# A two-layer decoder trunk on one core: transfers taken off ScalarE's queue, a fixed order for the sums of activations, and one product's loop order

## The chip, the cores and the metric

The kernel runs on one core of one Trainium2 chip. The metric is the device time of one execution in microseconds (us); of each kernel several executions are timed and the median is given. Beside these, one execution is recorded by the profiler; its span and trace are what is read below.

## The reference, cut to what matters

Two decoder layers are applied to a prompt of 1024 tokens and to 8 samples of 4 new tokens, together 1056 columns, with a model width of 1024.

- Layer 0 mixes tokens by attention in three dilated windows per head (12 pairs of head and window), whose outputs are combined by softmax denominators. Layer 1 mixes by a state space: the projected input u goes through 32 groups of 64 complex states and out again as y, then through a GELU and a gated product ("GLU").
- In both layers four heads of cross-attention read 256 memory tokens, and one output projection merges mixer and cross-attention into the residual x.
- Each layer ends in a gated FFN of width 2816, with a causal convolution of width 3 between up-projection and activation: `(silu(a) * b) @ w_down`.
- Everything is float32. Each dense product is made of three passes on TensorE, each operand split into a high part (a cast to fp32r) and a low part (the rest).

Outputs are the two activations, the new key and value windows, the new states and the convolution's last rows.

## The kernel before

**Engines and queues.** TensorE (PE) does all products and transposes. ScalarE (ACT) makes the high parts, exponentials and most copies out of PSUM; VectorE (DVE) the low parts, reductions and residual sums; GpSimd (POOL) some low parts and elementwise products. Each engine runs its instructions in the order in which the program lists them. Transfers are issued from three queues: SyncE (SP) issues weights and most reloads; POOL issues cache reads and window outputs; ACT issues what it has just written: attention outputs (`og`, `xm`, `xo`), the state space's output (`d_y`), states and convolution rows, 155 transfers in all. A transfer's issue stands in the engine's list like any instruction: what comes behind it waits until it is issued.

**Planner.** `Meter` (L112 to L198) keeps an estimated clock per engine while the program is written; `pump` (L329) moves pieces of side work, kept in 14 lanes, between the matmuls of the dense products when their inputs are estimated to be ready. So the order of each engine's list follows from estimated costs; a transfer on POOL is put at 1.0 us, on SP or ACT at 0.05 us.

**Attention (layer 0).** `scores` (L1138) works on two blocks at a time: scores on PE, maximum on DVE, exponential on ACT, transposes on PE, copies on ACT, product on PE, copy on ACT, then the write to `og`. `combine_head` reads `og` back, combines, and writes `xm`. `cross_p` and `cross_s` do cross-attention and write `xo`. Tiles S (14 buffers) hold the scores' data until the write has landed.

**State space (layer 1).** For each quarter m of the 32 groups, `s5_u_evac` (L1753) writes u to memory (`d_u`) and reads it back transposed into `s5u` in 8 transfers, both on SP. `s5_states` makes the states on PE, ACT copies them out of PSUM, DVE rotates and scans them; `s5_out` (L1821) makes y on PE, applies GELU on ACT and writes `d_y` in 8 transfers on ACT's queue. Between these, PE works on the cross-attention's projections. Four PSUM buffers (`pm`) serve the side work.

**FFN.** The first 3 of 22 tiles of the up-projection are made plainly, the others by a Strassen-like scheme with 7 products (`up_tiles`, L2160) that needs sums of quarters of the normalized activations: `t1`, `t2` (split into high and low), `t3`, `t4`. `up_moving` (L2065) makes the sums on DVE as side work of a lane, a step wherever the planner finds DVE free, in the stretch of the plain tiles. Product 0 uses unsummed activations, product 1 uses `t2` and product 2 adds to product 0's PSUM buffers, after ACT has copied product 0 out.

**Output projection.** `out_half` (L1918) makes 8 tiles of 128 rows; `dense` (L422) goes over three chunks of 352 columns with the k-blocks inside, or, with `along`, over the k-blocks with the chunks inside.

Of the kernel before, what the change touches and what calls it, by code (L numbers as in the profile page):

```python
# [10 lines left out]
F32 = mybir.dt.float32  # L11
# [3 lines left out]
ALU = mybir.AluOpType  # L15
AX = mybir.AxisListType

P = 128
# [93 lines left out]
class Meter:  # L112
# [51 lines left out]
    def note(self, eng, op, args, kw):  # L164
        outs = [kw[k] for k in ("out", "accum_out") if kw.get(k) is not None] or [args[0]]
        ins = list(args["out" not in kw:]) + [v for k, v in kw.items() if k not in ("out", "accum_out")]
        ins = [a for a in ins if hasattr(a, "tensor")]
        out = outs[0]
        n = out.free_size()
        src = next((a for a in ins if a.free_size() >= n), out)  # L170
        start = max(self.t[eng], self.ready(ins, eng), *(self.used.get(o.tensor.name, 0.0) if o.space == bass.MemoryType.PSUM else 0.0 for o in outs))
        if op == "dma_start":
            if out.space != bass.MemoryType.DRAM:
                start = max(start, self.t["tensor"] - 4.0)
            self.t[eng] = start + (1.0 if eng == "gpsimd" else 0.05)
            self.dma[eng] = max(self.dma.get(eng, 0.0), self.t[eng] + 1.6) + n * out.ap[0][1] * 4 / 350e3
            end = self.dma[eng] + 0.2
        else:
            if eng == "tensor":
                wide = ins[0].dtype == F32  # L180
                turn = op == "transpose"
                cost = 0.107 if turn else max(n * 4 / 2400 + 0.008, 0.107) + 0.03 if wide else max(n / 2400, 0.025) + 0.0025
            elif eng == "scalar":
                vecs = sum(hasattr(kw.get(x), "tensor") for x in ("scale", "bias", "accum_out"))
                cost = (0.051 if src.space == bass.MemoryType.PSUM else 0.094) + n * 0.833e-3 + 0.0935 * vecs
            elif eng == "gpsimd":
                cost = 0.147 + n * 2.105e-3
# [61 lines left out]
class Kernel:  # L249
# [661 lines left out]
    def cross_p(self, h, b0, q, a, done, kmt, kv, dst):  # L911
# [5 lines left out]
        for st in range(b0, b0 + 5):  # L917
# [18 lines left out]
            if st < b0 + 4:  # L936
# [9 lines left out]
                nc.scalar.copy(out=t, in_=p2[:, 0, :])  # L946
                self.m.let_go(p2)
                yield t
        nc.scalar.dma_start(out=dst[:, b0 * P:(b0 + 4) * P], in_=q[:, b0 * P:(b0 + 4) * P])
        self.crossed += 1  # L950

    def cross_s(self, l, qs, sqs, dst, ring_of, lane=None):
# [83 lines left out]
        o2 = self.M()  # L1036
        nc.scalar.copy(out=o2, in_=po[:, 0, :])
        for h in range(4):
            nc.scalar.dma_start(out=dst[h][:, NPR:], in_=o2[:, h * 32:(h + 1) * 32])
        self.crossed += 1  # L1040

    def cross_heads(self, lanes, heads, cq, kmt, kv, xo):
# [95 lines left out]
    def scores(self, g, h, part, qT, kT, vt):  # L1138
# [8 lines left out]
        for j in (part, part + 2):  # L1147
# [31 lines left out]
            nc.scalar.copy(out=o[:, :, 0:P], in_=po[:, 0:2, :])  # L1179
            self.m.let_go(po)  # L1180
            if g == 0:
                nc.scalar.dma_start(out=og.rearrange("(b p) x -> p b x", p=P)[:, 2 * j:2 * j + 2, :], in_=o)
            elif g == 1:
                nc.scalar.dma_start(out=og.rearrange("(e p r) x -> r p e x", p=P, r=4)[j], in_=o)
            else:
                v = og.rearrange("(l j e r) x -> r j l e x", j=4, e=2, r=2)
                for r in range(2):
                    nc.scalar.dma_start(out=v[r, j], in_=o[r * 64:(r + 1) * 64])
            del t, o
        self.scored[h] += 1  # L1190

# [6 lines left out]
    def combine_head(self, h, halves=(0, 1)):  # L1198
        while self.scored[h] < 6:
            yield WAIT  # L1200
        for i in halves:
            x01, x2 = self.combine_load(h, i)
            row = self.B((P, 512))
            yield DVE, x01, x2
            yield from self.combine(row, x01, x2)
            self.nc.scalar.dma_start(out=self.xm[h][:, i * 512:(i + 1) * 512], in_=row)
            del x01, x2, row
            self.scored[h] += 1

# [543 lines left out]
    def s5_u_evac(self, m, i, ps):  # L1753
# [23 lines left out]
        nc.sync.dma_start(out=win, in_=self.d_win[:, m * 4:m * 4 + 4])  # L1777
        nc.sync.dma_start(out=rot, in_=self.d_rot[:, m * 4:m * 4 + 4])
        for tau in range(8):
            nc.sync.dma_start(out=self.s5u[tau * 16:(tau + 1) * 16, m * 8:m * 8 + 8], in_=uv[tau][:, m * 8:m * 8 + 8])  # L1780
        self.lanes[0].append(self.s5_states(m, win, rot))

    def s5_states(self, m, win, rot):
# [37 lines left out]
    def s5_out(self, m, tl, cl):  # L1821
# [17 lines left out]
        nc.scalar.activation(out=y, in_=y, func=AF.Gelu_apprx_tanh)  # L1839
        yv = self.d_y.rearrange("(g c) t x -> t c g x", c=16)  # L1840
        for tau in range(8):
            nc.scalar.dma_start(out=yv[tau][:, m * 8:m * 8 + 8, :], in_=y[tau * 16:(tau + 1) * 16])
        self.s5_done += 1

    def s5_final(self):
# [20 lines left out]
        self.nc.tensor.transpose(ps[:32, 0, :], fin, self.ident)  # L1866
        po = self.M((32, P))
        nc.scalar.copy(out=po, in_=ps[:32, 0, :])
        nc.scalar.dma_start(out=self.O["p_s5"][0, 0].rearrange("r (i e) p -> (r i) (e p)", e=2), in_=po)
        for hf in range(2):  # L1870
            so = self.B((16, 8, P))
            for q in range(2):
                yield sf
                ps = self.pm((P, 4, P))
                for w in range(4):
                    self.nc.tensor.transpose(ps[:16, w, :], sf[:, hf * 8 + q * 4 + w].rearrange("p b r -> p (b r)"), self.ident)
                nc.scalar.copy(out=so[:, q * 4:q * 4 + 4, :], in_=ps[:16])
            nc.scalar.dma_start(out=self.O["s_s5"][0].rearrange("b r g p -> (b r) (g p)")[:, hf * D:(hf + 1) * D], in_=so.rearrange("p a b -> p (a b)"))

    def y_load(self, m):  # L1880
        y = self.B()
# [36 lines left out]
    def out_half(self, kt, aat, ahead=3, deep=1):  # L1918
        for m in range(8):
            self.wdeep = deep if m > 5 else 1  # L1920
            for j in range(m, min(m + ahead, 8)):
                self.reload_x(j)
            ps = self.dense_w(kt, aat)
            self.residual(m, ps)

    def cross_gather(self, xo, l):
# [85 lines left out]
    def conv_store(self, l):  # L2012
        nc = self.nc
        so = self.O["s_conv"][l].rearrange("b j c -> (b j) c")
        for q, last in ((0, 7), (3, 9), (1, 15), (4, 17), (2, 21), (5, 21)):
# [10 lines left out]
                nc.scalar.copy(out=r[:, hf * 4:hf * 4 + 4, :], in_=ps[:18])  # L2026
                self.m.let_go(ps)
            rv = r.rearrange("p a b -> p (a b)")
            nc.scalar.dma_start(out=so[:, q * D:q * D + n * P], in_=rv[0:16, :n * P])
            nc.scalar.dma_start(out=self.O["p_conv"][l, 0, :, q * D:q * D + n * P], in_=rv[16:18, :n * P])  # L2030
        self.cst = None

    def conv_sb(self, ct, u, out):
# [31 lines left out]
    def up_moving(self):  # L2065

        nc, y = self.nc, self.x
        tt = nc.vector.tensor_tensor
        L, R = slice(0, HT2), slice(HT2, NT)
        t1, t2 = self.mv = [self.L((P, 2, 4, HT2), F32R) for _ in range(2)]  # L2070
        for k in range(4):
            u, v = y[k], y[k + 4]
            yield DVE, u
            tt(out=u[:, L], in0=u[:, R], in1=u[:, L], op=ALU.subtract)
            nc.scalar.copy(out=t1[:, 0, k, :], in_=u[:, L])
            yield DVE
            tt(out=u[:, R], in0=v[:, R], in1=u[:, R], op=ALU.subtract)
            yield DVE
            tt(out=v[:, R], in0=v[:, R], in1=u[:, L], op=ALU.subtract)
            nc.scalar.copy(out=t2[:, 0, k, :], in_=v[:, R])  # L2080
            yield DVE
            tt(out=t1[:, 1, k, :], in0=u[:, L], in1=t1[:, 0, k, :].bitcast(F32), op=ALU.subtract)
            yield DVE
            tt(out=v[:, L], in0=v[:, L], in1=v[:, R], op=ALU.subtract)
            yield DVE
            tt(out=t2[:, 1, k, :], in0=v[:, R], in1=t2[:, 0, k, :].bitcast(F32), op=ALU.subtract)
        self.moving = True

    def up_raw(self, l, ht, s):
        if ht < NHT:  # L2090
# [69 lines left out]
    def up_tiles(self, l, weights):  # L2160
# [15 lines left out]

        def split_t3():
            for k in range(4):
                self.split_to(y[k][:, R], h0[:, k, R], l0[:, k, R])
                yield  # L2180

        def split_t4():
# [101 lines left out]
    def ffn(self, l, *side):  # L2284
        nc = self.nc
        first = [None] * 2
        self.hd, self.hid, self.uraw, self.uops, self.moving = {}, {}, {}, deque(), False
        self.wend = self.wi + 2 * PLAIN

        def evac(s, i, ps):  # L2290
# [7 lines left out]
                pass  # L2298

        h = self.norm_dense(FCG, evac)  # L2300
        self.lanes[1].append(self.up_moving())
        last(0, first)
        del first
        weights = self.up_weights(l)
# [1 line left out]
        for ht, s in ((ht, s) for ht in range(1, PLAIN) for s in range(2)):  # L2306
# [8 lines left out]
            for i in range(3):  # L2315
                ps = self.dense(8, lambda k: (hi[:, k, :], lo[:, k, :]), h, FCG[i:i + 1])[0]
                self.pump()
                if todo:
                    self.conv(*todo.pop())
                    if len(ab) == 3:  # L2320
                        last(ht - 1, (ab.pop(0), ab.pop(0)))
# [3 lines left out]
        del ab, ps, hi, lo  # L2325
        self.up_raw(l, PLAIN + 1, 1)
        h = None
        self.until(lambda: self.moving)
        late = self.up_tiles(l, weights)
        self.nh = None  # L2330
        for g in range(5):
# [287 lines left out]
```

## Time and profile before

| | |
|---|---|
| timed runs | 2921.52, 2922.92, 2925.99 us; median 2922.92 us |
| profiled execution | 2920.49 us, of which span 2918.7 us |
| mean granted TensorE clock | 0.971 of full speed |
| busy, share of the span | PE 94%, PEld 90%, DVE 70%, ACT 42%, POOL 13% |
| transfers | 431.56 MB, mean 148 GB/s |

The share of busy time tells which engine sets the time on average; what a change of one stage is worth is read from the waits in that stage. Times in the rows are in us from the span's start, unless they are marked ns. Nearly every instruction has line L216, since a helper issues it; groups are told apart by the tiles that they write and read (B<-pd is a tile B written from a PSUM tile pd).

### The profile page before, as it was taken

How to read it: one execution, taken by the hardware profiler on the slowest of the kernel's cores; microseconds unless marked ns; L12 is line 12 of the kernel's file. 1: busy time of each engine (PE TensorE's matmuls, PEld its weight loads, DVE VectorE, ACT ScalarE, POOL GpSimd, SP SyncE). 2: the span in 40 equal slices, each digit the busy share in tenths (PEclk: the TensorE clock that was granted, in tenths of full speed). 3: DMA queues.
4: the chain of work that ended last, by engine and by line, in shares of the span. 5: the costliest groups of instructions: out<-in, count | busy, mean ns of one | idle time of the engine just before them, and what ended most of it. 6: DMA issues, size and time to landing. Idle time of an engine off the chain costs nothing.

```text
span 2918.7 us, 50794 instructions
## 1 busy us (share of the span) xinstructions
PE 2734.6 (94%) x18896; PEld 2620.0 (90%) x18896; DVE 2055.1 (70%) x5933; ACT 1220.0 (42%) x3045; POOL 388.2 (13%) x571
## 2 busy tenths in 40 slices
PE   7999989999889999999999899888999999999999
PEld 5999878898878999999999888677999999999998
DVE  7466876887786787878769776545478787876444
ACT  5555555455441544444431124246244444443211
POOL 2100121112012400000102456000140000000000
PEclk8999999999989999999999999999999999999999
DMA  7234756757473423433564335853443233346421
GB/s 248 84 94 132 213 166 206 203 169 208 147 218 122 157 88 117 124 117 124 171 223 139 137 104 164 239 135 117 150 147 124 95 124 117 124 132 230 157 81 67
DMA packets 377348, 431.56 MB, mean 148 GB/s; under 512 B 31191, under 2 KB 331253, under 8 KB 375677
## 3 DMA queue, kind: packets, MB, share of 16 engines
q1 hardware_dynamic: 333212, 362.13, 39.0%
q0 software_dynamic: 20816, 50.04, 5.7%
q10 hardware_dynamic: 23072, 16.14, 2.0%
q8 instruction: 149, 2.44, 0.3%
q14 instruction: 99, 0.80, 0.1%
HBM read 345.10 MB, written 172.37 MB: 177 GB/s over the span
## 4 chain that ended last, share of the span: by engine, by line
PE 30%; DVE 22%; ACT 8%; issue 3%; DMA 2%; POOL 0%; ACTq 0%; SPq 0%; POOLq 0%; DVEq 0%
PE pd L216 26%; DVE B L216 18%; ACT B L216 5%; PE pm L216 4%; DVE S L216 3%; ACT S L216 1%; ACT L L216 1%; DVE A L216 0%; DMA B<-in_w_down 0%; DVE T L216 0%; DMA d_cl<-S 0%; DVE L L216 0%; ACT T L216 0%; ACT A L216 0%; DMA d_u<-M 0%
## 5 line engine op out<-in xcount | busy, mean ns | idle before, releaser
L216 PE MATMUL pd<-A,B 128*128 128x352 f32 (+2 forms) x10992 | 1791.2, 317 | 46.5 <-DVE B L216 31.0
L216 PEld LDWEIGHTS pd<-A,B 128*128 128x128 f32 x10992 | 1648.4, 191 | 74.9 <-issue 38.1
L216 DVE TENSOR_TENSOR B<-B,B 128x512 fp32r<-128x512 f32 (+7 forms) x612 | 514.5, 849 | 222.3 <-ACT B L216 212.2
L216 ACT CAST B<-B 128x512 fp32r<-128x512 f32 (+4 forms) x430 | 313.8, 751 | 671.7 <-DVE B L216 349.2
L216 PE MATMUL pd<-L,B 128*128 128x264 f32 (+1 forms) x2976 | 448.5, 303 | 14.1 <-DVE L L216 9.2
L216 PEld LDWEIGHTS pd<-L,B 128*128 128x128 f32 x2976 | 416.8, 190 | 18.1 <-DVE L L216 9.8
L216 DVE TENSOR_TENSOR B<-pd,B 128x352 f32<-128x352 f32 x408 | 203.0, 520 | 205.5 <-PE pd L216 198.2
L216 ACT COPY B<-pm 128x512 f32<-128x512 f32 (+5 forms) x261 | 129.7, 507 | 206.1 <-PE pm L216 203.0
L216 PE MATMUL pd<-B,B 128*128 128x264 f32 (+2 forms) x1308 | 205.5, 307 | 6.8 <-DVE B L216 6.8
L216 DVE SCALAR_TENSOR_TENSOR B<-B,S,B 128x1023 f32<-128x1023 f32 (+1 forms) x152 | 194.3, 1278 | 0.0
L216 PEld LDWEIGHTS pd<-B,B 128*128 128x128 f32 x1308 | 182.7, 191 | 11.1 <-ACT L L216 6.7
L216 PE MATMUL pm<-const,B 128*128 128x128 f32 (+6 forms) x1119 | 163.2, 276 | 26.7 <-DMA B<-in_g_mix 7.3
L216 PEld LDWEIGHTS pm<-const,B 128*128 128x128 f32 (+4 forms) x1119 | 132.4, 149 | 46.3 <-issue 17.3
L216 ACT COPY S<-pm 128x256 f32<-128x256 f32 (+5 forms) x278 | 89.1, 349 | 164.9 <-PE pm L216 154.5
L216 ACT COPY B<-pd 128x352 f32<-128x352 f32 (+4 forms) x211 | 104.2, 542 | 102.3 <-PE pd L216 95.2
L216 ACT CAST A<-B 128x352 fp32r<-128x352 f32 (+3 forms) x148 | 97.7, 669 | 114.0 <-DVE B L216 48.1
L216 ACT ACTIVATE B<-B 128x352 f32<-128x352 f32 (+3 forms) x127 | 94.3, 750 | 62.3 <-DVE B L216 58.5
L216 PE MATMUL pm<-const,S 128*128 128x128 f32 (+3 forms) x464 | 80.7, 283 | 33.6 <-ACT S L216 22.7
L216 DVE SCALAR_TENSOR_TENSOR L<-L,T,L 128x128 f32<-128x128 f32 x404 | 108.3, 346 | 4.0 <-DMA L<-in_cache_win_kv 3.9
L216 DVE CUSTOM_DVE_ANT_0 M<-L,L 128x128 f32<-128x128 f32 x384 | 94.6, 306 | 16.9 <-ACT M L216 6.1
L216 PEld LDWEIGHTS pm<-const,S 128*128 128x128 f32 (+2 forms) x464 | 58.3, 155 | 48.7 <-ACT S L216 30.2
L216 ACT ACTIVATE B<-B,S 128x1056 f32<-128x1056 f32 x76 | 96.7, 1273 | 2.4 <-DVE B L216 2.4
(217 smaller groups left out, 2503.1 us busy)
## 6 DMA issues: line engine op xcount, KB each, us to landing
B<-in_w_up SPq DMA_DIRECT2D x88, 512.0 KB
hd<-B SPq DMA_DIRECT2D x44, 528.0 KB
B<-hd SPq DMA_DIRECT2D x44, 528.0 KB
B<-in_w_down SPq DMA_DIRECT2D x44, 512.0 KB
B<-in_w_in_a SPq DMA_DIRECT2D x40, 512.0 KB
B<-xsp SPq DMA_DIRECT2D x32, 528.0 KB
L<-in_cache_win_kv SPq DMA_DIRECT2D x16, 1024.0 KB
L<-in_cache_win_kv SPq DMA_DIRECT2D x64, 256.0 KB
```

The costliest lines, as they stand in the source:

```text
L216: return f(*args, **kw)
```

## The change

Three things are changed, beside one cost of the planner (0.6 instead of 1.0 us for a transfer on POOL).

1. All 155 transfers of ACT's queue are issued by POOL. The reads of u into `s5u` (32) go from SP to POOL.
2. `up_moving` is no lane any more. It is stepped by the loop over the plain tiles, once after each of 12 dense products (the first step only takes the buffers, 8 steps work). `t3` is now formed from `t2`, and `t3` and `t4` are made on POOL (8 subtractions of 528 columns per layer). DVE keeps 16 of its 24; ACT's 8 copies stay.
3. The first tile of each `out_half` runs with `along`.

```diff
-            self.t[eng] = start + (1.0 if eng == "gpsimd" else 0.05)
+            self.t[eng] = start + (0.6 if eng == "gpsimd" else 0.05)
...
     # cross_p, cross_s, scores, combine_head, s5_out, s5_final, conv_store
-        nc.scalar.dma_start(out=dst[:, b0 * P:(b0 + 4) * P], in_=q[:, b0 * P:(b0 + 4) * P])
+        nc.gpsimd.dma_start(out=dst[:, b0 * P:(b0 + 4) * P], in_=q[:, b0 * P:(b0 + 4) * P])
...
     # s5_u_evac
         for tau in range(8):
-            nc.sync.dma_start(out=self.s5u[tau * 16:(tau + 1) * 16, m * 8:m * 8 + 8], in_=uv[tau][:, m * 8:m * 8 + 8])
+            nc.gpsimd.dma_start(out=self.s5u[tau * 16:(tau + 1) * 16, m * 8:m * 8 + 8], in_=uv[tau][:, m * 8:m * 8 + 8])
...
     # s5_out
         for tau in range(8):
-            nc.scalar.dma_start(out=yv[tau][:, m * 8:m * 8 + 8, :], in_=y[tau * 16:(tau + 1) * 16])
+            nc.gpsimd.dma_start(out=yv[tau][:, m * 8:m * 8 + 8, :], in_=y[tau * 16:(tau + 1) * 16])
...
     # out_half
-            ps = self.dense_w(kt, aat)
+            ps = self.dense_w(kt, aat, along=m == 0)
...
     # up_moving, inner part
+        yield
+        for step in ("a0", "a1 p0", "a2 p1", "a3 p2", "b0 p3", "b1", "b2", "b3"):
+            for w in step.split():
+                k = int(w[1])
+                u, v = y[k], y[k + 4]
+                if w[0] == "a":
+                    tt(out=u[:, R], in0=u[:, R], in1=u[:, L], op=ALU.subtract)
+                    tt(out=v[:, R], in0=v[:, R], in1=u[:, R], op=ALU.subtract)
+                    nc.scalar.copy(out=t1[:, 0, k, :], in_=u[:, R])
+                    nc.scalar.copy(out=t2[:, 0, k, :], in_=v[:, R])
+                elif w[0] == "p":
+                    nc.gpsimd.tensor_tensor(out=u[:, L], in0=v[:, R], in1=u[:, L], op=ALU.subtract)
+                    nc.gpsimd.tensor_tensor(out=v[:, L], in0=v[:, L], in1=v[:, R], op=ALU.subtract)
+                else:
+                    tt(out=t1[:, 1, k, :], in0=u[:, R], in1=t1[:, 0, k, :].bitcast(F32), op=ALU.subtract)
+                    tt(out=t2[:, 1, k, :], in0=v[:, R], in1=t2[:, 0, k, :].bitcast(F32), op=ALU.subtract)
+            yield
...
     # ffn: the lane and the wait for it go, the loop over the plain tiles steps the sums
-        self.lanes[1].append(self.up_moving())
+        moving = self.up_moving()
...
                 self.pump()
+                next(moving, None)
...
-        self.until(lambda: self.moving)
+        for _ in moving:
+            pass
```

## Rows read from the trace of the kernel before

**Rows 1.** Page, part 1: busy us, share of the span, instructions of each engine.

```profile
PE   2734.6 (94%) x18896; PEld 2620.0 (90%) x18896; DVE 2055.1 (70%) x5933; ACT 1220.0 (42%) x3045; POOL 388.2 (13%) x571
```

**Rows 2.** Waits of PE, longest group: waiting and awaited tile: us, times, longest.

```profile
PE pm L216 <- ACT S L216: 48.7, 26, 13.0
```

**Rows 3.** Stage table: us, busy us (instructions) of PE, PEld, DVE, ACT, POOL; clock; DMA.

```profile
100.00:920.00 820.00, 753.39 (x4898) 708.90 (x4898) 602.40 (x2898) 412.12 (x1305) 129.38 (x193) 0.96 0.57 169
...
1790.00:1935.00 145.00, 130.83 (x913) 117.99 (x912) 67.46 (x139) 45.15 (x118) 19.35 (x34) 0.94 0.71 194
```

**Rows 4.** Timeline of PE in the state space: start, us, instruction, [idle before <-releaser].

```profile
1869.59 5.09 PE L216 MATMUL pm<-L,B 128*128 128x144 f32 x24 [12.95 <-ACT S L216]
...
1875.20 2.72 PE L216 MATMUL pm<-L,B 128*128 128x144 f32 x24
```

**Rows 5.** Chain of waits, 1840 to 1890 us: start, us, what.

```profile
1847.95 7.54 DMA d_u<-M
...
1856.41 4.46 DMA L<-d_u
...
1860.95 3.83 DMA d_y<-L
...
1864.80 4.30 DMA B<-d_t
```

**Rows 6.** Timeline of ACT, the GELU ahead of the first writes of y.

```profile
1849.11 1.17 ACT L216 ACTIVATE L<-L 128x1152 f32<-128x1152 f32 x1
```

**Rows 7.** Timeline of POOL, its first instruction after 1812 us.

```profile
1937.41 2.86 POOL L216 DMA_DIRECT2D A<-in_cache_mem_kv  x4 [125.70 <-PE pd L216]
```

**Rows 8.** Groups of POOL: xcount | busy us, mean ns | idle before.

```profile
L216 POOL TENSOR_TENSOR A<-B,A 128x352 fp32r<-128x352 f32 (+1 forms) x73 | 77.7, 1090 | 87.2 <-ACT A L216 87.1
...
L216 POOL DMA_DIRECT2D d_ks<-S x16 | 8.5, 529 | 30.9 <-DVE S L216 30.9
```

**Rows 9.** Timelines of ACT and PE at the end of the attention.

```profile
851.70 3.16 ACTq L216 DMA_DIRECT2D og<-S  x2
...
856.42 0.71 PE L216 MATMUL pm<-const,S 128*128 128x128 f32 x2 [4.32 <-ACT S L216]
```

**Rows 10.** Tile og, its writes: xcount, ns min/median/max, first and last start.

```profile
L216 ACTq DMA_DIRECT2D og<-S x64: 366/582/1641, 168.6 to 869.4; - x64
```

**Rows 11.** Timeline of all engines where layer 0's products of sums begin.

```profile
1050.46 1.37 PE L216 MATMUL pd<-L,B 128*128 128x264 f32 x10
...
1054.71 0.70 DVE L216 TENSOR_TENSOR L<-B,L 128x528 fp32r<-128x528 f32 x1
...
1055.47 3.43 PE L216 MATMUL pd<-L,B 128*128 128x264 f32 x14 [3.64 <-DVE L L216]
...
1058.70 0.65 ACT L216 COPY S<-pd 128x264 f32<-128x264 f32 x2
...
1059.13 3.05 PE L216 MATMUL pd<-A,B 128*128 128x264 f32 x23 [0.23 <-ACT S L216]
```

**Rows 12.** The same place of layer 1, PE alone.

```profile
2241.93 2.48 PE L216 MATMUL pd<-L,B 128*128 128x264 f32 x14 [3.89 <-DVE L L216]
...
2245.60 6.61 PE L216 MATMUL pd<-A,B 128*128 128x264 f32 x36 [1.18 <-ACT S L216]
```

**Rows 13.** Timeline of DVE, two operations while POOL works.

```profile
847.64 2.95 DVE L216 CUSTOM_DVE_ANT_0 M<-L,L 128x128 f32<-128x128 f32 x1
...
993.28 1.21 DVE L216 SCALAR_TENSOR_TENSOR B<-pd,S,B 128x352 f32<-128x352 f32 x2 [0.31 <-ACT B L216]
```

**Rows 14.** Timeline of POOL beside the two.

```profile
847.96 2.47 POOL L216 TENSOR_TENSOR A<-B,A 128x1056 fp32r<-128x1056 f32 x1
...
989.82 6.69 POOL L216 TENSOR_TENSOR A<-B,A 128x352 fp32r<-128x352 f32 x7 [3.60 <-ACT A L216]
```

**Rows 15.** Timeline of PE in the first tile of layer 1's output projection.

```profile
2033.22 0.42 PE L216 MATMUL pd<-L,B 128*128 128x352 f32 x1 [1.48 <-ACT L L216]
2035.28 0.95 PE L216 MATMUL pd<-L,B 128*128 128x352 f32 x2 [1.64 <-DVE L L216]
```

More of the change, by code (lines that the diff above doesn't have):

```diff
@@ L1038, in cross_s @@
         for h in range(4):
-            nc.scalar.dma_start(out=dst[h][:, NPR:], in_=o2[:, h * 32:(h + 1) * 32])
+            nc.gpsimd.dma_start(out=dst[h][:, NPR:], in_=o2[:, h * 32:(h + 1) * 32])
         self.crossed += 1
@@ L1181, in scores @@
             if g == 0:
-                nc.scalar.dma_start(out=og.rearrange("(b p) x -> p b x", p=P)[:, 2 * j:2 * j + 2, :], in_=o)
+                nc.gpsimd.dma_start(out=og.rearrange("(b p) x -> p b x", p=P)[:, 2 * j:2 * j + 2, :], in_=o)
             elif g == 1:
-                nc.scalar.dma_start(out=og.rearrange("(e p r) x -> r p e x", p=P, r=4)[j], in_=o)
+                nc.gpsimd.dma_start(out=og.rearrange("(e p r) x -> r p e x", p=P, r=4)[j], in_=o)
             else:
@@ L1187, in scores @@
                 for r in range(2):
-                    nc.scalar.dma_start(out=v[r, j], in_=o[r * 64:(r + 1) * 64])
+                    nc.gpsimd.dma_start(out=v[r, j], in_=o[r * 64:(r + 1) * 64])
             del t, o
@@ L1205, in combine_head @@
             yield from self.combine(row, x01, x2)
-            self.nc.scalar.dma_start(out=self.xm[h][:, i * 512:(i + 1) * 512], in_=row)
+            self.nc.gpsimd.dma_start(out=self.xm[h][:, i * 512:(i + 1) * 512], in_=row)
             del x01, x2, row
@@ L1868, in s5_final @@
         nc.scalar.copy(out=po, in_=ps[:32, 0, :])
-        nc.scalar.dma_start(out=self.O["p_s5"][0, 0].rearrange("r (i e) p -> (r i) (e p)", e=2), in_=po)
+        nc.gpsimd.dma_start(out=self.O["p_s5"][0, 0].rearrange("r (i e) p -> (r i) (e p)", e=2), in_=po)
         for hf in range(2):
@@ L1877, in s5_final @@
                 nc.scalar.copy(out=so[:, q * 4:q * 4 + 4, :], in_=ps[:16])
-            nc.scalar.dma_start(out=self.O["s_s5"][0].rearrange("b r g p -> (b r) (g p)")[:, hf * D:(hf + 1) * D], in_=so.rearrange("p a b -> p (a b)"))
+            nc.gpsimd.dma_start(out=self.O["s_s5"][0].rearrange("b r g p -> (b r) (g p)")[:, hf * D:(hf + 1) * D], in_=so.rearrange("p a b -> p (a b)"))
     def y_load(self, m):
@@ L2028, in conv_store @@
             rv = r.rearrange("p a b -> p (a b)")
-            nc.scalar.dma_start(out=so[:, q * D:q * D + n * P], in_=rv[0:16, :n * P])
-            nc.scalar.dma_start(out=self.O["p_conv"][l, 0, :, q * D:q * D + n * P], in_=rv[16:18, :n * P])
+            nc.gpsimd.dma_start(out=so[:, q * D:q * D + n * P], in_=rv[0:16, :n * P])
+            nc.gpsimd.dma_start(out=self.O["p_conv"][l, 0, :, q * D:q * D + n * P], in_=rv[16:18, :n * P])
         self.cst = None
@@ L2070, in up_moving @@
         t1, t2 = self.mv = [self.L((P, 2, 4, HT2), F32R) for _ in range(2)]
[L2071 to L2087, printed above, removed]
+        yield
[15 more added lines that the diff above has]
+            yield
     def up_raw(self, l, ht, s):
@@ L2178, in split_t3 @@
             for k in range(4):
-                self.split_to(y[k][:, R], h0[:, k, R], l0[:, k, R])
+                self.split_to(y[k][:, L], h0[:, k, R], l0[:, k, R])
                 yield
@@ L2286, in ffn @@
         first = [None] * 2
-        self.hd, self.hid, self.uraw, self.uops, self.moving = {}, {}, {}, deque(), False
+        self.hd, self.hid, self.uraw, self.uops = {}, {}, {}, deque()
         self.wend = self.wi + 2 * PLAIN
```

## The prediction

> **What bounds the kernel now.** I read the busy shares first [rows 1]: PE is busy 2734.6 us of a span of 2918.7, so TensorE sets the time and 184 us, at most, are to be had from its waits. The waits of PE by what released them come next [rows 2]: the longest group, 48.7 us, waits for tiles S that ACT copies, and one wait of 13.0 us is more than a quarter of it. The stage table then says where PE is idle and at what clock [rows 3]: 66.6 us in the attention (100 to 920), 14.2 us in the state space (1790 to 1935), where the granted clock is 0.94. The timeline of PE in the state space shows one gap, 12.95 us ahead of 1869.59, and 24 matmuls after it that take 5.09 us where the next 24 of the same kind take 2.72 [rows 4]: the gap also costs 2.37 us of clock, in all 15.3 us.
>
> What held ACT there is read from the chain of waits [rows 5]. The small part of u is issued at 1847.95 and takes 7.54 us to land; then SP issues its reads of u, the second of them at 1856.41, landing 4.46 us later; only then is the first write of y issued, by ACT, at 1860.95. Its data had been ready since the GELU's end, 1849.11 + 1.17 = 1850.28 [rows 6]. A write of y does not need that read of another quarter; the chain ties ACT's queue to SP's transfers all the same, and the reverse: the write lands after 3.83 us, and SP's next load starts at 1864.80. I read it as completion flags that SP and ACT use in turn. ACT's copies that empty PSUM stand behind the eight writes, and PE behind the copies. So TensorE is bound here by a queue, not by work.
>
> **The change, part by part.** All sums are against the profiled execution, 2920.49 us; the median of the runs is 2.4 us above it, which I add at the end.
>
> *1. Writes of y and reads of u go to POOL.* ACT's copies then run when their matmuls end, PE's gap of 12.95 us goes, and with it the 2.37 us of clock: at most -15.3. The cover is POOL's idle stretch: 125.70 us without an instruction before 1937.41 [rows 7], against 64 transfers (32 each way) at about 0.53 us, the row of a write of similar small pieces [rows 8], 34 us. The writes of y for quarter 0 will stand on POOL behind the reads of quarter 3, which still wait for the landing at 1855.5; nobody but POOL waits there. What is late next is the states of quarter 3: their reads, eight at 0.53 us from 1855.5 on, are issued by 1859.7 and, with 4.46 us to land, are there at 1864.2. PE comes to those states behind the two groups of 24 matmuls of [rows 4], which ended at 1875.20 + 2.72 = 1877.92 and, 15.3 us earlier, end at 1862.6: 1.6 us too early, if nothing stood between. I leave 2.3 us for this and for the transfers that SP can now start sooner. Taken: -13; ends 0 (POOL's queue stalls PE in ACT's place) and -15.3.
>
> The Trainium skill, page "DMA: Bandwidth & Descriptors", section "Issuing engines are not separate DMA queues", says that starting transfers from several engines saves no more than the time the sequencer needs to start them. By that rule this part would be worth eight issues, some 5 us, and the whole sum 8 us less. This trace shows otherwise: 10.67 us pass between the data being ready and the first issue.
>
> *2. The other writes leave ACT.* At the attention's end two writes of og hold ACT 3.16 us from 851.70, and PE waits 4.32 us until 856.42 [rows 9]. The exponentials ahead of those transposes also wait for DVE, which was held until 850.6 and has more of the same work after it [rows 13]; so of 0 to -4.32 I take -2. In the rest of the attention 64 writes of og occupy ACT 0.58 us each [rows 10]. PE's waits for S tiles, without the two gaps above, are 31.4 us in 24 waits [rows 2]. If half of them lose one issue, it is 12 x 0.58 = 7; scores run beside dense products, so not each counts: -3, ends 0 and -7.
>
> *3. The sums of activations.* Layer 0 first [rows 11]. PE stops in product 1 because the last low part of t2 ends on DVE at 1055.4: 3.64 us; the 14 matmuls left take 3.43 us where 10 took 1.37 (so 14 should take 1.92): 1.51 us of clock; then 0.23 us. In all 5.4. In layer 1 [rows 12]: 3.89 and 1.18 us of waits, 2.48 - 1.92 = 0.56 and 6.61 - 36 x 0.1326 (23 in 3.05) = 1.84 of clock, in all 7.5. With the fixed order the sums are made at least three dense products before. But the wait does not vanish: product 2 adds to banks that ACT copies out at 1058.70, after high parts of t3 which follow, in ACT's list, work of DVE. DVE loses three sums right ahead of it (the one shown took 0.70, starts are some 0.62 apart: 1.86 us) and, I take, as much in the steps before, which delay the last convolution; the copy then comes 3.7 us earlier, at 1055.0, and product 2 at 1055.4, while product 1 would end at 1051.83 + 1.92 = 1053.75. So 1.7 us of waiting stay, and layer 0 gains 3.7. Layer 1 gains 4.0, by the same shift, and 1.84 of clock. Sum -9.5, taken -9; ends -12.9 (all waits go) and 0.
>
> The eight subtractions that POOL takes cost about 1.24 us each (1056 columns took 2.47 [rows 14]), 10 us per layer, in a stretch where POOL is idle. They can hold DVE: one operation with two inputs in SBUF took 2.95 us beside POOL's 2.47, while a convolution step that reads PSUM kept 0.6 us each beside POOL [rows 13, 14]. Each pair of POOL's starts when its own inputs are made, and DVE's next step of this kind is a dense product (4.5 us) later, so I cost it at nothing; the ends are 0 and +20 for both layers.
>
> The Trainium skill says, on "SBUF — State Buffer" under "Who interferes with whom", that a VectorE instruction with two inputs in SBUF and a GpSimd instruction that reads SBUF exclude one another for their whole length. The rows agree (2.95 against 2.47). By this rule alone the sums on GpSimd work against the change; it is rival B.
>
> *4. The first tile with the k-blocks outside.* In layer 1 PE waits 1.48 and 1.64 us for the last k-block's parts [rows 15]; with 27 matmuls of the earlier blocks ahead instead of 9, at about 0.19 us each, 3.4 us more cover: -3, ends 0 and -3.1. In layer 0 the like is part of the gap of 4.32, counted above. The three PSUM banks taken at once can cost an eviction's wait, counted in 5.
>
> *5. What POOL gets.* 155 + 32 transfers at 0.53 us are 99 us on an engine busy 388 us [rows 1, 8]. In the attention, 88 of them (47 us) stand among POOL's 129 us of work [rows 3], some of it on the way to the combined heads. Twelve steps of combining, each late by one issue, are 6 us; with the banks of part 4 at most +10; I take +3. The planner's changed costs move other work too, with either sign; I take no mean for it.
>
> Sum: -13 - 2 - 3 - 9 - 3 + 3 = -27, from 2920.5 to 2893.5, and as a median 2896.
>
> **The rivals.**
>
> *A. POOL's queue takes over ACT's wait.* In the state space the writes of y wait behind the reads of u, and y or the states arrive late, so that part 1 keeps only issue time (8 x 0.58 = 4.7 by [rows 10]), and part 2's -3 is lost too: 2896 + 8.3 + 3 = 2907. For it: the landing of 7.54 us stays in the chain [rows 5]. Against: the copies that free PSUM, for which PE waited, are no longer behind any transfer.
>
> *B. The sums on POOL hold DVE.* Then part 3 becomes -9 + 20 = +11, and the time 2916, no change. For it: 2.95 us [rows 13]. Against: the steps are spread over twelve products.
>
> *C. Slower: the scores' tiles come free later.* A write of og on POOL stands behind POOL's own waits; its S tiles stay taken, DVE's next masked maximum, which writes an S tile, waits in DVE's list, and the residual sums that empty PE's banks behind it. The price is 64 writes times the delay that reaches PE; at 0.63 us it is +40, and the time 2936. It decides from 27 / 64 = 0.42 us per write on. For it: PE's 66.6 idle us in this stretch are already waits of such chains. Against: POOL is busy only 129 of 820 us there [rows 3].
>
> *D. All ends come true:* -15.3 - 4.3 - 7 - 12.9 - 3.1 = -42.6, time 2880.
>
> **How the numbers follow.** Forecast 2896, with its own range 2886 to 2904: 0.53. A: 0.16. D and what lies towards it: 0.13. B: 0.08. C: 0.10. A measurement of this kernel can tell a difference from about 0.2%, 5.8 us: faster means under 2917.1. The forecast, A and D are faster, 0.82; B is the same, 0.08; C is slower, 0.10. The range of 2879 to 2915 leaves out C, B and a little of D.
>
> **What would show it.** Right: no PE wait over 3 us between 1840 and 1880, ACT's copies of the states within 1 us of their matmuls, reads of u on POOL from the landing on; the last low part of t2 some 10 us before product 1, and a wait of 1 to 2 us for ACT ahead of product 2, the clock at full speed behind it; no wait in the first tile of layer 1's projection; ACT busy as long as before, without its issues. Wrong: a gap of PE that ends with a transfer issued by POOL, DVE operations of 2 us or more in the plain tiles, or PE's idle time between 100 and 920 grown beyond 90 us.

## The result and the profile after

The changed kernel takes 2887.23 us (median of 4 runs, 2876.76 to 2892.83), the kernel before 2922.22 us beside it (4 runs, 2916.21 to 2925.99). The ratio is 0.9879, with a 95% interval of 0.9856 to 0.9903: 35 us faster, between 28 and 42. The forecast was 2896, its own range 2886 to 2904. The profiled execution takes 2884.84 us, its span 2883.1.

The page's first part, against [rows 1]: PE is busy 21 us less for the same 18896 matmuls, ACT as long as before, and POOL 129 us more for 202 more instructions.

```profile
PE   2713.7 (94%) x18896; PEld 2601.1 (90%) x18896; DVE 2047.9 (71%) x5918; ACT 1216.7 (42%) x3045; POOL 517.6 (18%) x773
```

PE's waits by releaser, against [rows 2]: the group that led before is halved and its longest wait is 3.4 us instead of 13.0. Two other groups now hold the longest waits, 7.9 and 7.8 us.

```profile
PE pd L216 <- DVE B L216: 50.3, 48, 7.9
PE pm L216 <- ACT S L216: 25.1, 23, 3.4
PE pm L216 <- ACT B L216: 24.2, 14, 7.8
```

The stage table with the same two stretches of work, against [rows 3] (the second by some 20 matmuls longer). The attention takes 804 us instead of 820, the state space 138 instead of 145. In the attention PE's idle time is hardly shorter (64.0 against 66.6); what shrank is the time of its matmuls, at a slightly higher granted clock (0.97 against 0.96).

```profile
98.00:902.00 804.00, 739.97 (x4900) 698.53 (x4900) 598.48 (x2898) 411.56 (x1307) 181.48 (x278) 0.97 0.59 172
1770.00:1908.00 138.00, 130.71 (x936) 118.49 (x935) 67.29 (x139) 45.27 (x120) 44.42 (x79) 0.98 0.75 201
```

The state space, timelines of PE, ACT and POOL, against [rows 4 to 7]. Where a group of 24 matmuls took 5.09 us behind the stop, none takes more than 2.78. ACT's copy of the states comes 3.56 us after the GELU because PE is not ready, not because ACT is held. POOL issues reads and writes. It does wait in turn, once 4.33 us for a landing of u ahead of a write of y, but no wait of PE ends with that write. One thing is worse: the reads of the first quarter (issued from 1792.12 on, the last there at 1803.94) land late and PE waits 5.59 us for a transfer that POOL issued, which I had named as a sign that I was wrong.

```profile
1792.12 4.23 POOL L216 DMA_DIRECT2D L<-d_u  x8 [7.31 <-DMA d_u<-M]
...
1804.24 1.18 PE L216 MATMUL pm<-L,B 128*64 128x136 f32 x8 [5.59 <-DMA L<-d_u]
...
1847.67 0.53 POOL L216 DMA_DIRECT2D d_y<-L  x1 [4.33 <-DMA L<-d_u]
...
1849.54 1.17 ACT L216 ACTIVATE L<-L 128x1152 f32<-128x1152 f32 x1
1854.28 0.38 ACT L216 COPY L<-pm 128x256 f32<-128x256 f32 x1 [3.56 <-PE pm L216]
...
1861.85 2.78 PE L216 MATMUL pm<-L,B 128*128 128x144 f32 x24
```

The end of the attention, against [rows 9]: no write between ACT's copy and its exponentials, and PE waits 1.61 us where it waited 4.32. Some 15 us earlier stands a new wait, the 7.89 us of the list above. POOL writes scores of the samples to memory at 808.67 and reads them back from 814.45 on; VectorE comes to them in its list 4.54 us before they land, and a low part for PE is behind them.

```profile
808.67 0.56 POOL L216 DMA_DIRECT2D scr<-S  x1 [0.93 <-DVE S L216]
...
814.45 1.81 POOL L216 DMA_DIRECT2D L<-scr  x3 [4.71 <-DMA scr<-S]
...
822.51 0.29 DVE L216 CUSTOM_DVE_ANT_0 M<-L,L 128x128 f32<-128x128 f32 x1 [4.54 <-DMA L<-scr]
...
825.91 5.06 PE L216 MATMUL pd<-B,A 128*128 128x512 f32 x11 [7.89 <-DVE B L216]
...
839.76 0.40 ACT L216 ACTIVATE S<-S,T 128x128 f32<-128x128 f32 x1 [1.51 <-DVE T L216]
...
840.30 0.71 PE L216 MATMUL pm<-const,S 128*128 128x128 f32 x2 [1.61 <-ACT S L216]
```

The products of sums, against [rows 11, 12]: no wait ahead of product 1 (24 matmuls in 3.08 us), but one of 2.28 ahead of product 2 in either layer, after which layer 0's 48 matmuls take 7.54 us (granted clock 0.78) where layer 1's take 6.11 (1.00); and a new one, 1.05 us, for a low part 15 us earlier.

```profile
1023.88 14.57 PE L216 MATMUL pd<-A,B 128*128 128x352 f32 x94 [1.05 <-DVE B L216]
1038.28 3.08 PE L216 MATMUL pd<-L,B 128*128 128x264 f32 x24
...
1041.09 2.23 ACT L216 CAST A<-B 128x528 fp32r<-128x528 f32 x4
1043.22 0.65 ACT L216 COPY S<-pd 128x264 f32<-128x264 f32 x2
...
1043.64 7.54 PE L216 MATMUL pd<-A,B 128*128 128x264 f32 x48 [2.28 <-ACT S L216]
...
2212.00 6.11 PE L216 MATMUL pd<-A,B 128*128 128x264 f32 x48 [2.28 <-ACT S L216]
```

To place the gain I number the 15,360 matmuls of the dense products (those into pd with 264 columns or more), which come in the same order in every kernel here, and subtract start from start. By before's times: 300 to 760, +8.4 us (lost); 760 to 923, -24.0; 923 to 996, +4.3 (granted clock 0.93 instead of 1.00); layer 0's sums (996 to 1075), -0.6; state space and the cross-attention's products (1768 to 1911), -13.4; on to layer 1's projection (2042), -6.0; layer 1's sums (2220 to 2260), -4.4. Kernels with the same lists up to a point differ there by up to 7 us in such a sum, so of single stretches only the repeated ones count.

### The profile page after: what moved, and what is told of

The parts are those of the page before. It is cut to its first block, busy times and chain, and to the rows that moved or that the text cites. A ratio compares the mean times of both kernels' runs of the same rounds, so it can differ in the third digit from the quotient of the medians.

```text
span 2883.1 us, 50916 instructions
## 1 busy us (share of the span) xinstructions
PE 2713.7 (94%) x18896; PEld 2601.1 (90%) x18896; DVE 2047.9 (71%) x5918; ACT 1216.7 (42%) x3045; POOL 517.6 (18%) x773
## 3 DMA queue, kind: packets, MB, share of 16 engines
q8 instruction: 149, 2.44, 0.4%
## 5 line engine op out<-in xcount | busy, mean ns | idle before, releaser
L216 ACT CAST A<-B 128x352 fp32r<-128x352 f32 (+3 forms) x148 | 97.0, 668 | 109.7 <-DVE B L216 45.5
L216 ACT ACTIVATE B<-B 128x352 f32<-128x352 f32 (+3 forms) x127 | 94.2, 750 | 50.7 <-DVE B L216 45.5
L216 DVE CUSTOM_DVE_ANT_0 M<-L,L 128x128 f32<-128x128 f32 x384 | 88.6, 290 | 27.1 <-DMA L<-scr 12.9
L216 POOL DMA_DIRECT2D out_s_conv<-B x12 | 6.2, 513 | 553.3 <-ACT B L216 553.3
```

Source lines behind the costliest of these rows:

```text
L216: return f(*args, **kw)
```

## The experiments

Each is given as its edit, the expectation on record, and the ratio to the kernel before that ran beside it (5 rounds; us worked out as 1 less the ratio, times that kernel's median). Parts of the change come first, one by one on the kernel before.

**Writes of y and reads of u alone.**

```diff
+            nc.gpsimd.dma_start(out=self.s5u[...], in_=uv[tau][...])
+            nc.gpsimd.dma_start(out=yv[tau][...], in_=y[...])
```

> The kernel before with one part of the change: the writes of y and the reads of u are issued by GpSimd; all else as before. Theory (SP's and ACT's transfers hold one another up): the whole 13 us that the state space gained between the two kernels come from here, so about 2909 us; the stop of PE of 12.95 us at 1856 shrinks to 6 us or less, the copies of the states follow their matmuls, and the half-speed matmuls behind the stop go. Rival (only the issuing time of the eight writes is saved): 5 us, about 2917, and a stop of PE of 8 us or more stays. Rival A of the prediction (GpSimd's queue takes over the wait): no gain, and a wait of PE that ends with a transfer issued by GpSimd.

Ratio 0.9953 (0.994 to 0.9967): -13.7 us (-9.6 to -17.5). PE's waits of over 1 us between 1800 and 1900 are 1.84, 1.11 and 1.91 us, the last two for loads of d_t and d_cl. The rival of issuing time alone, priced at the eight writes of one quarter (-5), is out of the interval; all 32 writes, at the 0.44 us that the median one took before, are 14 us of ACT, which the time alone does not exclude.

**The sums alone** (the loop and the steps as in the change).

> The kernel before with the fixed steps for the sums of activations alone. The prediction's term: -9 us, 2913 (layer 0 -3.7, layer 1 -5.8). What the two traces show when the same products are set beside each other: -0.6 in layer 0 and -4.2 in layer 1, about -5, 2917, with a wait of PE of about 2 us ahead of product 1 or 2 of layer 0 still there. Rival B (the subtractions on GpSimd hold VectorE): 2922 or more, with VectorE operations of 2 us or more in the plain tiles.

Ratio 0.9982 (0.9972 to 0.9991): -5.3 us (-2.6 to -8.2), not the -9 of the prediction. Rival B is out: beside POOL's subtractions VectorE's operations are longer by 0.2 to 0.3 us (0.96 where 0.70 is usual, 1.43 where 1.22 is), not by 2.

```profile
1012.63 1.33 POOL L216 TENSOR_TENSOR B<-B 128x528 f32<-128x528 f32 x1
...
1013.57 0.96 DVE L216 TENSOR_TENSOR B<-B 128x528 f32<-128x528 f32 x1
...
1016.71 1.35 POOL L216 TENSOR_TENSOR B<-B 128x528 f32<-128x528 f32 x1
...
1017.71 1.43 DVE L216 TENSOR_TENSOR B<-B,B 128x1024 fp32r<-128x1024 f32 x1
```

The Trainium skill, "SBUF — State Buffer", "Who interferes with whom", has a VectorE instruction with two inputs in SBUF and a GpSimd instruction that reads SBUF exclude one another. The rows agree: the first pair overlaps for 0.39 us and VectorE's operation is 0.26 us longer. The overlap is short because the steps are a dense product apart.

**The loop order alone.**

```diff
+            ps = self.dense_w(kt, aat, along=m == 0)
```

> The kernel before with the new loop order of the first tile of each output projection alone. Between the two kernels the stretch from the attention's end to the end of the output projection (760 to 920 us) became 21.6 us shorter, where 2 were predicted. Theory L (the loop order does it: more matmuls stand ready while the last transposes and exponentials are waited for): 15 to 20 us faster, about 2904, most of it before 923 us, and the waits of 1.5 us in layer 1's first tile gone. Theory W (the writes that left ACT, or the order that the planner then writes, do it): the loop order gives 3 us in layer 1 and 2 to 4 in layer 0, about 2916.

Ratio 0.9977 (0.9966 to 0.9987): -6.7 us (-3.8 to -9.9). Its trace gains 7.7 us between 850 and 923 and 2.7 in layer 1. Neither theory's size fits; the 24 us are not mainly its doing.

**The other writes with the planner's cost, and the cost alone.**

```diff
-            self.t[eng] = start + (1.0 if eng == "gpsimd" else 0.05)
+            self.t[eng] = start + (0.6 if eng == "gpsimd" else 0.05)
```

> The kernel before with the other writes (og, xm, xo, final states, convolution rows) issued by GpSimd and the planner's cost of 0.6 us; reads of u, writes of y, the sums and the loop order as before. Theory W (these writes and the order that the planner then writes give the 21.6 us of the stretch 760 to 920, and lose the 5.4 us of the stretch 100 to 760): about 16 us faster, 2906. Theory L (the loop order gives the 21.6): this kernel is 0 to 5 us slower than the kernel before, 2922 to 2927. The prediction had -5 +3 for this part: 2920.

> The kernel before with the planner's cost of a transfer on GpSimd at 0.6 us instead of 1.0, nothing else; the order of PE's list differs from the kernel before from the attention on. Theory O (the order that the planner writes gives the 21 us of the stretch 760 to 920 that the run with the other writes and this cost showed): 10 to 17 us faster, 2901 to 2908, with 760 to 920 shorter by 15 or more. Theory Q (the queue gives them, since ACT's list is free of transfers): within 5 us of before, 2913 to 2922, and 760 to 920 as long as before.

Together 0.9949 (0.9936 to 0.9962), -14.9 us, with -21.2 in 760 to 923, as theory W has it. The cost alone, which moves no transfer to another queue, gives 0.9968 (0.9958 to 0.9978): -9.3 us (-6.4 to -12.3), just short of theory O's -10, with -13.3 in 760 to 923. So more than half is the order that the planner writes. The difference, some 5.6 us (0.8 to 10.3), is the writes and what the planner, which now books them on POOL, changes in the order for them: the two kernels' lists differ. The long wait of PE after the memory round trip is in the order, too; here it is without any moved write:

```profile
829.63 4.15 PE L216 MATMUL pd<-B,A 128*128 128x512 f32 x11 [7.93 <-DVE B L216]
```

The other writes at the old cost were not tried.

**The queue with the order held.** The changed kernel's lists, but the other writes go back to ACT's list while the planner books them on POOL.

```diff
+    as_pool = lambda self, **k: (self.note("gpsimd", "dma_start", (), k), self.nc.scalar.dma_start(**k))
...
-                nc.gpsimd.dma_start(out=og..., in_=o)
+                nc.as_pool(out=og..., in_=o)
```

> The changed kernel with the other writes (og, xm, xo, final states, convolution rows) issued by ScalarE again, but planned as if GpSimd issued them, so that PE, VectorE and SyncE have the changed kernel's lists to the last instruction. Theory O (the order gives the gain at the attention's end): 760 to 920 stays short, the time is the changed kernel's within 5 us, 2877 to 2888; the wait of 7.8 us at 376, where VectorE waits for products of GpSimd that stand behind its transfers, goes (5 us faster) if that wait comes of the moved writes. Theory Q (the queue gives it): 2895 to 2905, with waits of PE for ACT back at the attention's end.

Ratio 0.9919 (0.9907 to 0.9931): -23.6 us, so the writes' place is worth about 12 of the changed kernel's 35, with an interval of 4 to 19; the lists of PE, VectorE and ScalarE are the changed kernel's to the last instruction. Theory O's 5 is at the low end of that, and the two theories share the gain. Where the 12 lie is only in part shown: in the two traces 760 to 923 differs by 7.0 us (-24.0 against -17.0), and 923 to 996 gives 4.2 of them back, because there the changed kernel's clock is 0.93 and this one's 1.00. The wait at 376 is still there with 7.92 us: it is not of the moved writes. The wait at the attention's end is back, and this time nothing but a write explains it: the exponential follows the second pair of writes of og. Of the 4.30 us, 3.1 are not issuing: the second write waits from 843.25 to 846.37 for the landing of a weight load of SyncE, with which it shares a completion flag (more on these flags under step 1 below).

```profile
842.67 4.30 ACTq L113 DMA_DIRECT2D og<-S  x2
847.02 0.40 ACT L216 ACTIVATE S<-S,T 128x128 f32<-128x128 f32 x1 [5.05 <-DMA og<-S]
...
847.57 0.86 PE L216 MATMUL pm<-const,S 128*128 128x128 f32 x2 [5.57 <-ACT S L216]
```

**The changed kernel without the other writes, planned so.**

> The changed kernel with the other writes issued by ScalarE and planned so: reads of u and writes of y on GpSimd, the sums, the loop order and the cost of 0.6 us stay. By the single parts (-13.6 for y and u, -5.3 for the sums, -6.7 for the loop order) it is 26 us faster than before, 2892, if the cost alone does nothing (theory Q); with theory O some 10 to 17 more, 2875 to 2882, and without the 6.5 us that the changed kernel loses between 300 and 500.

Ratio 0.9897 (0.9883 to 0.9912): -30.1 us. With an order of its own ACT's writes cost 5 us, within the error of 8. Theory Q's -26 lies in the interval of -25.7 to -34.1 and theory O's -36 to -43 does not, although the cost alone gave -9.3 on the kernel before: the parts do not simply add.

**Reads of u alone, writes of y alone.**

```diff
+            nc.gpsimd.dma_start(out=self.s5u[...], in_=uv[tau][...])   # first kernel
+            nc.gpsimd.dma_start(out=yv[tau][...], in_=y[...])          # second kernel
```

> The kernel before with the reads of u issued by GpSimd; the writes of y stay on ScalarE. Theory F (ACT's issue of the first write waited for SP's reads of u, through completion flags that the two queues use in turn): the wait of ACT of 10.67 us shrinks to 4 us or less and PE's stop of 12.95 us to 6 or less; 8 to 13 us faster, 2905 to 2910, although ACT still issues all writes. Rival I (what counts is that ACT issues): no gain, 2917, ACT still waits 8 us or more. A middle case: ACT now waits for the landing of the small part of u (7.54 us), which SP still issues; then half, 5 us.

> The kernel before with the writes of y alone issued by GpSimd; the reads of u stay on SyncE. With the reads of u alone moved, ACT's issue of the first write of y followed the GELU at once (its wait of 10.67 us was gone), but the state space gained only 3 us: SyncE still waited 45.5 us for writes of y and its loads of d_t and d_cl came late. Theory F (two queues hold one another up through flags that they use in turn): with the writes gone from ACT both sides are free, so nearly all of the 13.6 us of the two edits together comes back, 9 to 13 us, 2905 to 2909, and SyncE's waits for writes of y go. Rival: each edit needs the other (SyncE's eight reads behind the landing of u hold its loads); 2 to 5 us, 2913 to 2916.

The reads alone: 0.9992 (0.998 to 1.0004), no change that can be told. Yet the mechanism of theory F is plain in the trace: the GELU ends at 1854.54 and ACT issues at 1854.57, where [rows 5, 6] had 10.67 us between. The gap went and the time did not. PE now waits for loads that SyncE issues late, and its matmuls behind the waits are slow (20 in 3.85 us, at a granted clock of 0.50; the same 20 of the next quarter take 2.50).

```profile
1853.37 1.17 ACT L216 ACTIVATE L<-L 128x1152 f32<-128x1152 f32 x1
1854.57 4.38 ACTq L216 DMA_DIRECT2D d_y<-L  x8
...
1863.28 0.73 PE L216 MATMUL pm<-L,B 128*128 128x144 f32 x4 [2.39 <-DMA B<-d_t]
1864.92 3.85 PE L216 MATMUL pm<-L,B 64*128 64x144 f32 x20 [0.91 <-DMA B<-d_cl]
```

The kernel with the writes alone has much the same waits, so they are not what keeps the gain away:

```profile
1868.69 1.30 PE L216 MATMUL pm<-L,B 128*128 128x144 f32 x4 [2.60 <-DMA B<-d_t]
1870.38 3.85 PE L216 MATMUL pm<-L,B 64*128 64x144 f32 x20 [0.39 <-DMA B<-d_cl]
```

What does differ is how long SyncE waits between 1780 and 1940 (waiting queue and awaited transfer: us, times, longest), here the kernel with the reads alone:

```profile
SPq L216 <- DMA d_y<-L: 45.5, 5, 22.4
```

and the one with the writes alone (1775 to 1935):

```profile
SPq L216 <- DMA d_y<-L: 4.8, 1, 4.8
```

The writes alone give 0.9949 (0.9929 to 0.9969), -14.9 us: all that both edits give. The four kernels make a square: moving the writes gains 14.9 us with the reads on SP and, from 0.9992 to 0.9953, 11.4 (6 to 17) with the reads on POOL; moving the reads gains nothing measurable in either row. The writes' gain is the queue's and not the order's: with and without it the lists of VectorE and ScalarE are the same, and PE's but for six matmuls. Of SyncE's 45.5 us, 43.5 are for writes that its next transfer does not need (the last 2.0 are ahead of the reload of y), and half, the longest wait, stands ahead of a load for which no PE wait is listed; the 4.8 us that are left with the writes on POOL are all ahead of the reload of y. So ACT's writes held SyncE, which does not need them, as SyncE's reads held ACT.

The prediction made 5 us of the Trainium skill's rule that a second issuing engine saves issuing time only ("DMA: Bandwidth & Descriptors", "Issuing engines are not separate DMA queues"), counting the eight writes of one quarter; 32 writes at 0.55 us (4.38 / 8) are 17.6, so the time alone does not refute the rule. Against it stand the 10.67 us without an issue, and that in the kernel with the reads alone, where ACT still issues all 32, PE's waits for ACT between 1780 and 1940 come to only 1.8 us. How much of the 14.9 is ACT's issuing time and how much SyncE's delay was not separated.

**Three attempts at the waits that are left**, all on the changed kernel: the planner's latency of reads on POOL at 4.0 us, the parts of t3 and t4 listed one product later, and both.

```diff
-            self.dma[eng] = max(self.dma.get(eng, 0.0), self.t[eng] + 1.6) + ...
+            self.dma[eng] = max(self.dma.get(eng, 0.0), self.t[eng] + (4.0 if eng == "gpsimd" and out.space != bass.MemoryType.DRAM else 1.6)) + ...
...
-                if ht == PLAIN and j == 0:      # split_t3
+                if ht == PLAIN and j == 1:
-                if ht == PLAIN and j == 2:      # split_t4
+                if ht == PLAIN and j == 3:
```

> The changed kernel, the planner's latency of a transfer that GpSimd issues into SBUF at 4.0 us instead of 1.6 (the trace of the changed kernel shows 5 to 8 us from issue to landing for the reads of the samples' scores). Theory D (the two longest waits of the attention, 7.83 us at 376 and 7.89 us at 818, are VectorE standing in its list at a copy of scores whose reads have not landed, with a low part or a maximum for PE behind it): both shrink to 3 us or less and the kernel is 8 to 12 us faster than the changed one, about 2877. Rival P (a new cost moves all the attention's work and other waits come up, as with the cost of 0.6 us alone): within 5 us of the changed kernel, 2882 to 2892, with other waits of 4 us and more in the attention.

Ratio 0.9896 (0.9875 to 0.9917), no gain over the changed kernel. Both waits of 7.8 us went as theory D has it, and others came up as rival P has it, 6.07, 6.02 and 5.86 us. The stretch 300 to 760 is 14.8 us shorter than the changed kernel's, 760 to 923 is 19.6 longer.

```profile
396.53 0.69 PE L216 MATMUL pm<-const,S 128*128 128x128 f32 x2 [6.07 <-ACT S L216]
...
539.19 1.11 PE L216 MATMUL pm<-const,B 128*128 128x128 f32 x4 [6.02 <-DVE B L216]
```

> The changed kernel, in which the high and low parts of t3 and t4 are listed one product later, so that ACT's copies of product 0 stand ahead of them. Theory S (what is left of the sums' gain is lost ahead of product 2, because its banks are copied out behind the four high parts of t3, 2.23 us, and the clock falls behind this wait: 48 matmuls in 7.54 us where 5.97 are usual): the waits of 2.28 us ahead of product 2 in both layers go, with 1.4 us of clock each, 7 us in all, about 2880. Rival: product 3 then waits for the low parts of t3 and nothing is gained, 2887.

Ratio 0.9894 (0.9873 to 0.9915), no gain either. The wait ahead of product 2 falls from 2.28 to 0.15 us and the granted clock behind it stays at 1.00, so theory S is right about the cause; but product 3 now waits 1.27 us, for VectorE, and the stretch of layer 0's sums gains 2.1 us, not 3.7.

```profile
1048.97 3.17 PE L216 MATMUL pd<-A,B 128*128 128x264 f32 x24 [0.15 <-ACT S L216]
1053.40 3.15 PE L216 MATMUL pd<-A,B 128*128 128x264 f32 x24 [1.27 <-DVE S L216]
```

> The changed kernel with the two edits that were run one by one: the planner's latency of 4.0 us for reads on GpSimd, and the parts of t3 and t4 listed one product later. Alone they gave ratios of 0.9896 and 0.9894 to the kernel before, the changed kernel 0.9879 (0.9856 to 0.9903). Theory: the later listing is worth the 2.1 us of layer 0 and 0.5 us of layer 1 that its trace showed, on top of the other edit's time: 0.988 to 0.989, about 2882, and no measurable difference from the changed kernel. A version that beats it would have to come out under 0.9856.

Ratio 0.9875 (0.985 to 0.99), as expected not told apart from the changed kernel's 0.9879. No version measurably beats it.

## Why the prediction was right in the sum and not in its parts

| step | predicted | measured |
|---|---|---|
| 1. writes of y, reads of u | -13 | -13.7 (-9.6 to -17.5) |
| 2 and 5. other writes off ACT, and what POOL pays | -2 - 3 + 3 = -2 | -5.6 on before, -5 and -12 on the changed kernel (each with an error of 5 to 8) |
| 3. sums | -9 | -5.3 (-2.6 to -8.2) |
| 4. loop order | -3 | -6.7 (-3.8 to -9.9) |
| the planner's cost | 0 | -9.3 (-6.4 to -12.3) |
| sum | -27 | -40.6; the whole change -35 (-28 to -42) |

*Step 1* held in size by the timed runs. Its own trace shows less of it in place: 6.3 us from 1768 to 1911 and 2.5 on to 2042; the rest of the 12.8 by which that span is shorter lies where nothing was moved. The coupling that I read from the chain is in the record, for the trace keeps the number of the flag (a semaphore) that each transfer sets when it has landed. SP and ACT share eight, 108 to 115, and take them in turn; POOL has eight of its own, 99 to 106. The first write of y carries flag 112 and waits for the flag's last holder, the third read of u (the one of 1856.41, which I called the second), there at 1860.87; SP's load of d_t at 1864.80 carries 112 again and waits for that write.

Two sentences of the step did not hold. I took the reads of u for the culprit because the chain showed one ahead of the first write; moving them alone frees ACT's first issue and gains nothing, moving the writes alone gains all. And I put 4.46 us to the landing of the reads; among the changed kernel's denser transfers (DMA share 1.04 between 1800 and 1850, 0.82 before) they take 8.1 us, the last figure of this row of its transfers from 1790 to 1940:

```profile
L<-d_u POOLq DMA_DIRECT2D x32, 72.0 KB, 8.1
```

The wait of 5.59 us, for the first quarter's reads, is the result, but not of the queue alone. With both edits and the old order PE waits 1.84 us there; with the new order and all reads on SP (the kernel with the cost alone) 2.86:

```profile
1808.91 1.18 PE L216 MATMUL pm<-L,B 128*64 128x136 f32 x8 [2.86 <-DMA L<-d_u]
```

So it is rival A's late states only in part. The last quarter's states, which I had 1.6 us too early for their reads, wait 1.70. And 2.9 of the 13.4 us in that stretch are not this step's: in the kernel with the cost alone a wait of 4.4 us for a low part on POOL at 1771 shrinks to 1.50 and 0.58, and the stop of 12.95 us itself to 2.44 and 3.97, with no transfer moved. The length of that stop belonged to the order as well as to the queue, and was no measure of what the queue costs.

*Step 2.* Of the 4.32 us at the attention's end I took half, because the exponentials also wait for DVE. The kernel with the order held shows 4 us for it (5.57 against 1.61): in that order VectorE's part was ready at 843.2 and the write came last in nearly all of the wait. In the kernel before VectorE's part was ready only at 854.4, 1.5 us ahead of the exponential at 855.88, so there half was no bad reading. What the step had wrong is the price of a write: it counted issuing, 0.58 us, where a write also waits for its flag, 3.1 us in the case shown above. POOL's 88 transfers in the attention cost nothing that shows: with the writes back on ACT the stretch 300 to 760 is as long (+10.4 against +8.4), so what is lost there is order. So rival C, which needed writes of og to come late on POOL, did not happen; PE's idle time from 100 to 920 stayed under the 90 us that would have told of it.

*Step 3* failed in layer 0. The wait ahead of product 1 went with its clock (-5.15 us) as predicted. I left 1.7 us ahead of product 2 at full clock; it is 2.28, and behind it the granted clock falls to 0.78 in layer 0 (7.54 against 6.11 us, the term I had at nothing), and VectorE's new steps make a weight's low part 1.05 us late. What stays is 0.6 us instead of 3.7. Layer 1 gains 4.4 where 5.8 were forecast.

*Step 4* was right for layer 1 (2.7 us against 3). In layer 0 I had it inside the wait of 4.32; but the first tile is what PE works on during all of the last scores, and two waits behind it, 2.38 and 3.74 us, counted as well: from 850 to 915 the waits sum to 10.4 us before (4.32 + 2.38 + 3.74) and to 5.7 with the loop order alone (0.48 + 2.18 + 0.38 + 2.65).

*The planner's cost* is the term that was not there: "I take no mean for it". A mean of nothing was the best guess without the changed lists, but it had a size, and it is larger than any single edit but the first. The terms' errors are -0.7, -3.6, +3.7, -3.7 and -9.3, in sum -13.6; the whole change is 5 us less than its parts, which is inside their intervals. That 2896 came within 9 us of 2887 is in part luck: it left out a term of 9.3 us, and the step of the sums gave 3.7 less than forecast. The range held the time because its lower end came from rival D, with terms larger than mine, and not because the missing term had been seen.

## What to carry to other kernels

Where two queues take turns at a few completion flags, look at what the second queue would do with a free first one before crediting a gap to the transfer ahead of it, and try each side alone: here moving the reads gained nothing and moving the writes gained all. In a kernel whose order a planner writes, a changed cost is an edit of its own and wants a run of its own; hold the order (book as one engine, issue on another) to price a queue. A memory round trip that a planner books too short shows up as an idle in-order engine with unrelated work behind it; lengthening one such figure moves the waits and need not shorten the sum.

## What the runs showed of the hardware that was not expected

- SP's and ACT's transfers took eight completion flags in turn, and an issue waited for its flag's last holder: writes on ACT's queue held transfers of SyncE's queue for 45.5 us in 160, of which data tied only 2.0. With the writes on GpSimd's queue, which has eight flags of its own, 4.8 us were left, all of them tied by data.
- Reads of u took 8.1 us from issue to landing in the changed kernel's state space, against 4.46 for the one in [rows 5], with the transfers' share of time up from 0.82 to 1.04.
- The first read of scores from memory in the changed kernel's long wait took 8.0 us from issue to landing (814.45 to 822.49), after 5.2 us from the issue of their write to its landing (808.67 to 813.91).
